# A hybrid decoder layer on one core: recurrence gates issued further behind their pair and one by one, and the silu gate's bank copied out before the sigmoid reads it

## The chip, the cores and the metric

The kernel runs on 1 core of one Trainium2 chip. The metric is the device time of one execution in microseconds (us); the times of a kernel are the median of several runs. One more execution was recorded by the hardware profiler, and its trace is what the views below read. The engines are TensorE (PE, with its weight load PEld), VectorE (DVE), ScalarE (ACT), GpSimd (POOL) and SyncE (SP, which issues nearly all DMAs).

## What is computed

One decoder layer on x (2048 x 1024) and 256 memory tokens, in float32. The reference, cut to the recurrence, which the change touches:

```python
hn = rms_norm(x, g_pre)
proj = hn @ w_in
rg_x, rg_g, da_q, da_k, da_v, da_g, xa_q, xa_g = jnp.split(proj, cuts, axis=-1)

xc = causal_depthwise_conv(rg_x, conv_w, conv_b)
r = sigmoid(xh @ w_rg_a + b_rg_a)
i = sigmoid(xh @ w_rg_x + b_rg_x)
log_a = -LRU_C * r * softplus(-lru_lambda)
u = sqrt(maximum(1 - exp(2 * log_a), 0)) * (i * xc)
h = scan(a * h + u)
y_rg = h * silu(rg_g)
...
y = jnp.concatenate([y_rg, y_da, y_xa], axis=-1) @ w_out
x = x + rms_norm(y, g_post)
```

Here xh is xc by heads. The other two groups are a differential attention (y_da) and a cross-attention into the memory tokens (y_xa), each times a silu gate.

## The kernel before, in words

Every float32 product is made of three matmuls (`mm3`, L197 through `mm`): each operand is split into a high part that TensorE's format holds and the low rest, and high x high, low x high and high x low are added in one PSUM bank. The function `split_weight` (L237, L238) does this for weights: ACT casts, POOL or DVE subtracts.

The 2048 tokens are four chunks of 512. The input projection (`project`, matmuls into tiles named `ip`) goes through 16 pairs of column blocks in two passes: chunks 0 and 1 in the first, chunks 2 and 3 in the second. A pair has four steps of 24 matmuls: for each of the two chunks one half and then the other. The tile `ip` lies in a PSUM pool of two banks, so a step needs the bank of the step before the last to be read out. In a recurrence pair ("rg", one for each of four blocks of 128 columns) the first half is the recurrence's input and the second its silu gate. In the first pass the four recurrence pairs come last, one after the other; in the second pass they alternate with attention pairs at places 1, 3, 5 and 7. So there are 16 places, one for each block and chunk.

After a step `ev_rg` takes the bank. For the first half ACT copies it (`xr`, L545), DVE runs the convolution of width 4 (`xc`, L550 and three times L553) and casts its high part (`xchl`, L556), and POOL subtracts to get the low part (L557). For the second half, the gate, ACT makes a sigmoid of three passes (Exp, Ln, Exp; L259 to L261) into `rgg`, and DVE multiplies it with the bank (L563). Then the generator `rg_gates` is handed to a list of streams. It makes the two recurrence gates: for each, three matmuls into a tile `rgo` from `xchl` and the split gate weights, and a sigmoid into `ri`. Then follow the recurrence's elementwise steps on ACT, POOL and DVE with a scan (L590), the multiply with `rgg` (L593) and a store that is issued 11 us later.

TensorE's order is the order in which the program issues its matmuls. It is set by a counter: `now[0]` grows by 512/2400 us for each matmul of 512 columns, streams carry a due time on that counter, and `pump`, called after every three projection matmuls, lets the due ones issue. `spawn(gen, delay)` puts a generator on the list, and each value that a generator yields is its next delay. The constant `RGW` is the delay between the end of a gate step and the first recurrence gate. The attention's streams (`s`, `pt`, `pthl`, `o`) and the transposes of the next rows (`xt`, `hnT`) run on the same list. For the other engines the framework sets the order, from priorities (`tc.high_priority`) and its own estimate of times; each engine then works through its list strictly in order, and what an instruction needs from another engine is a wait.

The `f2` tiles, among them `xr`, `xc`, `rgg`, the new `rgz` and the attention's `q2`, share nine buffers.

Of the kernel before, what the change touches and what calls it, by code (L numbers as in the profile page):

```python
# [18 lines left out]
CH = 512  # L19
# [12 lines left out]
S_GAP, SS_WAIT = 1.2, 6.25  # L32
XT_GAP, X1W = 1, 3.17
SQ0, SQ1, SQ_GAP = 0.1, 1.12, 1.39
RGW, XAW, XAT = 1.94, 1.77, 6.23

PRIO, PRS, PRX, PRN, PRM, PRR = 1000, 500, 500, 60, 261, -200
N_E = 12
# [19 lines left out]
def hybrid_layer(  # L58
# [13 lines left out]
    nc = tc.nc  # L72
# [16 lines left out]
    def f4(name, shape=(128, 1024), dt=F32, pool=p4):  # L89
        return pool.tile(list(shape), dt, tag="f4", name=name)  # L90

    def f2(name, shape=(128, 516), dt=F32, pool=p2):
        return pool.tile(list(shape), dt, tag="f2", name=name)
# [7 lines left out]
    def ps_s(name, shape=(128, 512)):  # L101
        return psS.tile(list(shape), F32, tag="S", name=name)
# [7 lines left out]
    def asf(ap):  # L110
        return ap.bitcast(F32)
# [92 lines left out]
    def spawn(gen, delay=0.0):  # L204
        streams.append([now[0] + delay, gen])

    def store(fn, delay):

        def go():
            fn()  # L210
            return
            yield
        spawn(go(), delay)
# [14 lines left out]
    def drain(cond=None):  # L228

        pump()  # L230
        while streams and not (cond is not None and cond()):
            now[0] = max(now[0], min(st[0] for st in streams))
            pump()
# [6 lines left out]
    def mm3(o, wh, wl, xh, xl, first, last):  # L240
        mm(o, wh, xh, first, False)
        mm(o, wl, xh, False, False)
        mm(o, wh, xl, False, last)
# [13 lines left out]
    def sigmoid(o, z, nb=0.0):  # L257

        nc.scalar.activation(o, z, AF.Exp, scale=-1.0, bias=nb)  # L259
        nc.scalar.activation(o, o, AF.Ln, bias=1.0)  # L260
        nc.scalar.activation(o, o, AF.Exp, scale=-1.0)  # L261
# [199 lines left out]
    def store_y(g, k, c, y):  # L461
        nc.sync.dma_start(YD[g][c][:, :, k, :].rearrange("t p k -> p t k"),
                          y.rearrange("p (t k) -> p t k", k=128))
# [64 lines left out]
    def rg_weights():  # L528
        raw = f4("rgraw", (128, 1024))
        nc.sync.dma_start(raw, w_rg)  # L530
        state["rgh"] = f4("rgh", (128, 4, 2, 128), F32R)
        state["rgl"] = f4("rgl", (128, 4, 2, 128), F32R)
        split_weight(raw, state["rgh"].rearrange("p a b c -> p (a b c)"),
                     state["rgl"].rearrange("p a b c -> p (a b c)"))

    def ev_rg(b, c, which, o):
        if which == 0:
            if c % 2:
                drain(lambda: not state["xa_live"])
            xr = f2("xr")  # L540
            if c == 0:
                nc.gpsimd.memset(xr[:, 0:3], 0.0)
            else:
                nc.gpsimd.tensor_copy(xr[:, 0:3], halo[:, b, :])
            nc.scalar.copy(xr[:, 3:515], o)  # L545
            if c < NCH - 1:
                nc.gpsimd.tensor_copy(halo[:, b, :], xr[:, 512:515])
            xc = f2("xc")
            cw = 4 * b
            nc.vector.tensor_scalar(xc[:, 0:CH], xr[:, 0:CH], vec2[:, cw:cw + 1], vec2[:, V_CB + b:V_CB + b + 1],  # L550
                                    op0=ALU.mult, op1=ALU.add)
            for k in range(1, 4):
                nc.vector.scalar_tensor_tensor(xc[:, 0:CH], xr[:, k:k + CH], vec2[:, cw + k:cw + k + 1],  # L553
                                               xc[:, 0:CH], op0=ALU.mult, op1=ALU.add)
            xh = f4("xchl", (128, 2, CH), F32R)
            nc.vector.tensor_copy(xh[:, 0], xc[:, 0:CH])  # L556
            nc.gpsimd.tensor_sub(xh[:, 1], xc[:, 0:CH], asf(xh[:, 0]))  # L557
            state["xc"] = xc, xh
            return
        xc, xh = state.pop("xc")  # L560
        gs = f2("rgg", (128, CH))
        sigmoid(gs, o)
        nc.vector.tensor_mul(gs, o, gs)  # L563
        state["rg_live"] = state.get("rg_live", 0) + 1
        spawn(rg_gates(b, c, xc, xh, gs), RGW)

    def rg_gates(b, c, xc, xh, gs):
        while state["xa_live"]:
            yield 0.5
        if "rgh" not in state:  # L570
            rg_weights()
            yield 5.0
        ri = f4("ri", (128, 2, CH))
        for g in range(2):
            o = ps_s("rgo")
            mm3(o, state["rgh"][:, b, g, :], state["rgl"][:, b, g, :], xh[:, 0], xh[:, 1], True, True)
            with tc.high_priority(offset=PRX):
                sigmoid(ri[:, g, :], o, nbias[:, 4 * g + b:4 * g + b + 1])
        with tc.high_priority(offset=PRR):
            r, i = ri[:, 0, :], ri[:, 1, :]  # L580
            a = f2("rga", (128, CH))
            nc.scalar.activation(a, r, AF.Exp, scale=nsp8[:, b:b + 1])
            nc.scalar.activation(r, r, AF.Exp, scale=nsp16[:, b:b + 1])
            nc.gpsimd.tensor_mul(i, i, xc[:, 0:CH])

            nc.vector.tensor_scalar(r, r, 1.0, 1.0, op0=ALU.min, op1=ALU.subtract)
            nc.scalar.activation(r, r, AF.Ln, scale=-1.0, bias=tinyb)
            nc.scalar.activation(r, r, AF.Exp, scale=0.5)
            nc.gpsimd.tensor_mul(i, i, r)
            nc.vector.tensor_tensor_scan(r, a, i, 0.0 if c == 0 else carry[:, b:b + 1], op0=ALU.mult, op1=ALU.add)  # L590
            if c < NCH - 1:
                nc.gpsimd.tensor_copy(carry[:, b:b + 1], r[:, CH - 1:CH])
            nc.vector.tensor_mul(r, r, gs)  # L593
        state["rg_live"] -= 1
        store(lambda: store_y(0, b, c, r), 11.0)
# [353 lines left out]
    def get_y(tt, grp):  # L949
        if (tt, grp) not in grans:  # L950
            drain(lambda: y_ready(tt, grp))
            grans[tt, grp] = y_granule(tt, grp)
        return grans[tt, grp]

    for tt in range(NT):
# [6 lines left out]
        for half, grp in order:  # L962
            cs = slice(half * 512, half * 512 + 512)
            g, wt = get_y(tt, grp), wout[grp]
            if os[half] is None:
                os[half] = ps_m("po")
            o = os[half]
# [82 lines left out]
```

## Time and profile before

| what | value |
|---|---|
| median of 3 runs | 1487.51 us (1486.01 to 1487.62) |
| the profiled execution | 1490.95 us |
| its span, first to last instruction | 1489.1 us |
| mean granted TensorE clock | 0.986 of 2.4 GHz |
| busy: PE / PEld | 1422.1 / 1208.6 us |
| busy: DVE / ACT / POOL | 918.4 / 811.5 / 563.8 us |
| DMA | 184.05 MB, 124 GB/s on average |

Busy time is the sum of an engine's instructions; on an engine that waits in line it says nothing of when. A list of waits shows for each line what ended the idle time before it. Matmuls overlap, so a row of the timeline with many of them gives their common duration. The granted clock is a share of 2.4 GHz, averaged over a stretch; the two levels are 1.2 and 2.4 GHz.

### The profile page before, as it was taken

The page shows a single profiled execution, that of the slowest core. Times are in us where ns is not written, and L with a number is a line of the kernel's source. Part 1 is how long each engine was busy: PE and PEld are TensorE (multiplying, and loading weights), DVE is VectorE, ACT ScalarE, POOL GpSimd, SP SyncE. Part 2 cuts the span into 40 slices and gives each one's busy share as a digit, 9 for nine tenths or more (in the row PEclk, how much of TensorE's full clock was granted, in tenths as well). Part 3 has the DMA queues.
Part 4 walks back from the last instruction along what each step waited for, and adds up shares of the span by engine and source line. Part 5 has one row for each costly group of instructions (what it writes and reads, how often), then busy time and mean ns, then how long its engine had stood idle before and what let it go on. Part 6 is the DMA issues. An engine that isn't in the chain of part 4 may idle for free.

```text
span 1489.1 us, 21951 instructions
## 1 busy us (share of the span) xinstructions
PE 1422.1 (95%) x7568; PEld 1208.6 (81%) x7568; DVE 918.4 (62%) x1862; ACT 811.5 (54%) x1972; POOL 563.8 (38%) x634
## 2 busy tenths in 40 slices
PE   5999999999998899899998999999999999999997
PEld 4789889888886678787786898888877888888886
DVE  6332565677545776757648576767778777777222
ACT  6343545666458674755556555666566545554221
POOL 2231433443446543535425343423346433334221
PEclk9999999999999899999999999999999999999999
DMA  6666666342322146244222543221375234322231
GB/s 218 162 214 219 177 172 206 99 132 82 106 68 64 50 128 187 72 151 123 84 68 71 163 141 128 68 85 40 116 237 174 86 133 151 103 96 76 99 123 70
DMA packets 138655, 184.05 MB, mean 124 GB/s; under 512 B 11440, under 2 KB 81200, under 8 KB 138544
## 3 DMA queue, kind: packets, MB, share of 16 engines
q1 hardware_dynamic: 138400, 182.64, 39.6%
q8 instruction: 59, 0.97, 0.3%
q14 instruction: 52, 0.43, 0.1%
q10 hardware_dynamic: 144, 0.01, 0.0%
HBM read 125.99 MB, written 56.62 MB: 123 GB/s over the span
## 4 chain that ended last, share of the span: by engine, by line
PE 74%; DVE 8%; ACT 6%; POOL 5%; issue 4%; DMA 2%; SPq 0%; DVEq 0%; POOLq 0%; ACTq 0%
PE ip L197 35%; PE po L197 17%; PE s L197 7%; PE o L197 6%; PE pt L201 4%; DVE e L719 2%; PE xas L197 2%; PE kv L197 1%; POOL e L718 1%; PE xao L197 1%; POOL wp L238 1%; DMA wraw<-in_w_in_dram 1%; PE rgo L197 1%; DVE xc L553 1%; ACT e L695 1%
## 5 line engine op out<-in xcount | busy, mean ns | idle before, releaser
L197 PE MATMUL ip<-hnT,wp 128*128 128x512 f32 x2688 | 676.8, 397 | 4.9 <-DVE rgg L563 4.9
L197 PEld LDWEIGHTS ip<-hnT,wp 128*128 128x128 f32 x2688 | 499.0, 190 | 105.8 <-DVE rgg L563 6.1
L695 ACT ACTIVATE e<-s,nm 128x512 f32<-128x512 f32 (+3 forms) x320 | 200.0, 625 | 233.4 <-DVE nm L693 216.3
L238 POOL TENSOR_TENSOR wp<-wraw,wp 128x512 fp32r<-128x512 f32 x133 | 182.2, 1380 | 201.8 <-ACT wp L237 192.8
L693 DVE TENSOR_REDUCE nm<-s 128x1 f32<-128x512 f32 (+3 forms) x320 | 193.2, 605 | 32.4 <-PE s L197 27.7
L197 PE MATMUL po<-wout,yg 128*128 128x512 f32 x768 | 193.5, 393 | 4.2 <-POOL wout L238 1.9
L718 POOL TENSOR_SCALAR e<-e,f 128x512 f32<-128x512 f32 (+3 forms) x160 | 120.3, 767 | 171.1 <-DVE f L714 93.5
L197 PE MATMUL s<-kv,q 128*128 128x512 f32 (+3 forms) x640 | 182.8, 367 | 1.0 <-ACT e L695 0.9
L197 PEld LDWEIGHTS po<-wout,yg 128*128 128x128 f32 x768 | 141.3, 188 | 34.3 <-POOL wout L238 3.3
L719 DVE SCALAR_TENSOR_TENSOR e<-e,f 128x512 f32<-128x512 f32 (+3 forms) x160 | 142.7, 919 | 28.5 <-POOL e L718 28.3
L197 PE MATMUL o<-pthl,kv 128*128 128x256 f32 (+1 forms) x864 | 136.3, 293 | 2.0 <-DVE pthl L760 2.0
L760 DVE TENSOR_TENSOR pthl<-pt,pthl 128x512 fp32r<-128x512 f32 (+1 forms) x144 | 94.6, 657 | 70.4 <-ACT pthl L759 70.0
L197 PEld LDWEIGHTS s<-kv,q 128*128 128x128 f32 x640 | 114.6, 189 | 21.8 <-ACT e L695 1.3
L197 PEld LDWEIGHTS o<-pthl,kv 128*128 128x128 f32 x864 | 116.1, 192 | 5.6 <-DVE pthl L760 2.8
L238 POOL TENSOR_TENSOR yg<-yraw,yg 128x512 fp32r<-128x512 f32 x48 | 64.2, 1341 | 133.1 <-ACT yg L237 122.0
L237 ACT CAST wp<-wraw 128x512 fp32r<-128x512 f32 x144 | 88.2, 618 | 43.9 <-PE ip L197 22.1
L759 ACT CAST pthl<-pt 128x512 fp32r<-128x512 f32 (+1 forms) x144 | 80.8, 561 | 53.3 <-PE pt L201 52.7
L197 PE MATMUL ip<-wp,hnT 128*128 128x256 f32 x768 | 99.4, 284 | 0.0
L197 PE MATMUL po<-wo,yg 128*128 128x512 f32 x384 | 97.3, 392 | 0.0
L197 PEld LDWEIGHTS ip<-wp,hnT 128*128 128x128 f32 x768 | 96.2, 192 | 1.2
L201 PE MATMUL pt<-ident,e 128*128 128x128 f32 x544 | 84.4, 276 | 5.6 <-DVE pthl L760 5.6
L201 PEld LDWEIGHTS pt<-ident,e 128*128 128x128 f32 x544 | 67.9, 142 | 20.8 <-DVE pthl L760 6.0
(183 smaller groups left out, 1731.2 us busy)
## 6 DMA issues: line engine op xcount, KB each, us to landing
wraw<-in_w_in_dram SPq DMA_DIRECT2D x128, 256.0 KB, 2.7
q<-QD SPq DMA_DIRECT2D x128, 128.0 KB, 3.3
kv<-KD SPq DMA_DIRECT2D x24, 512.0 KB, 5.7
kv<-VD SPq DMA_DIRECT2D x24, 512.0 KB, 5.0
yraw<-YD SPq DMA_DIRECT2D x48, 256.0 KB, 2.7
QD<-qkhl SPq DMA_DIRECT2D x32, 256.0 KB, 3.3
KD<-qkhl SPq DMA_DIRECT2D x32, 256.0 KB, 3.7
VD<-vhl SPq DMA_DIRECT2D x32, 256.0 KB, 2.8
```

The lines of the kernel that those rows point to most:

```text
L197: nc.tensor.matmul(o, w, xx, start=start, stop=stop)
L201: nc.tensor.transpose(o, i, ident)
L237: nc.scalar.copy(hi, raw)
L238: eng.tensor_sub(lo, raw, asf(hi))
L553: nc.vector.scalar_tensor_tensor(xc[:, 0:CH], xr[:, k:k + CH], vec2[:, cw + k:cw + k + 1], xc[:, 0:CH], op0=ALU.mult, op1=ALU.add)
L693: nc.vector.tensor_reduce(out=nm[:, c, kc:kc + 1], in_=s[:, 0:w], op=ALU.max, axis=AX.X, negate=True)
L695: nc.scalar.activation(e[kc, c][:, 0:w], s[:, 0:w], AF.Exp, bias=nm[:, c, kc:kc + 1], accum_out=l[:, c, kc:kc + 1])
L718: nc.gpsimd.tensor_scalar(e2, e2, f[:, 1, kc:kc + 1], 1.0, op0=ALU.mult, op1=ALU.mult)
L719: nc.vector.scalar_tensor_tensor(e1, e1, f[:, 0, kc:kc + 1], e2, op0=ALU.mult, op1=ALU.add)
L759: nc.scalar.copy(hi[:, 0:n], t[:, 0:n])
L760: nc.vector.tensor_sub(lo[:, 0:n], t[:, 0:n], asf(hi[:, 0:n]))
```

## The change

The first recurrence gate is issued after a delay of 5.0 instead of 1.94 on the counter, the second one after a further 1.4 instead of directly behind the first. The gate's bank is copied by DVE into a new SBUF tile `rgz`, and the multiply of the silu reads that copy and runs on POOL instead of DVE. Nothing else is edited; lines behind L563 move down by 1 to 3.

```diff
-RGW, XAW, XAT = 1.94, 1.77, 6.23
+RGW, RGG, XAW, XAT = 5.0, 1.4, 1.77, 6.23
...
         xc, xh = state.pop("xc")
-        gs = f2("rgg", (128, CH))
+        gs, z = f2("rgg", (128, CH)), f2("rgz", (128, CH))
+        nc.vector.tensor_copy(z, o)
         sigmoid(gs, o)
-        nc.vector.tensor_mul(gs, o, gs)
+        nc.gpsimd.tensor_mul(gs, z, gs)
         state["rg_live"] = state.get("rg_live", 0) + 1
         spawn(rg_gates(b, c, xc, xh, gs), RGW)
...
         ri = f4("ri", (128, 2, CH))
         for g in range(2):
+            if g:
+                yield RGG
             o = ps_s("rgo")
```

The change moves instructions on all engines. First TensorE, at the second recurrence pair of the first pass, second chunk. Before, six matmuls of two gates stand together behind twelve matmuls of the next step (`ip` with the buffer number of that step):

```order
L197 MATMUL ip_5155<-hnT01_318,wp_5012 128x512
L197 MATMUL rgo_5171<-xchl_5086,rgh_4787 128x512
L197 MATMUL rgo_5171<-xchl_5086,rgl_4788 128x512
L197 MATMUL rgo_5171<-xchl_5086,rgh_4787 128x512
L197 MATMUL rgo_5178<-xchl_5086,rgh_4787 128x512
L197 MATMUL rgo_5178<-xchl_5086,rgl_4788 128x512
L197 MATMUL rgo_5178<-xchl_5086,rgh_4787 128x512
L197 MATMUL ip_5155<-hnT00_317,wp_5096 128x512 x2
```

Now the first gate's three stand behind all 24 matmuls of that step, and a new `ip` tile begins behind them:

```order
L197 MATMUL ip_5163<-hnT01_318,wp_5118 128x512
L197 MATMUL rgo_5195<-xchl_5073,rgh_4801 128x512
L197 MATMUL rgo_5195<-xchl_5073,rgl_4802 128x512
L197 MATMUL rgo_5195<-xchl_5073,rgh_4801 128x512
L197 MATMUL ip_5219<-hnT00_317,wp_4958 128x512 x2
L197 MATMUL ip_5219<-hnT01_318,wp_4958 128x512
```

The first gate moved by twelve matmuls; the second one follows nine `ip` matmuls further on.

Second, DVE at the same place (`xc` is the convolution, `xrow` the rows of the next chunk, scaled by their norm). Before:

```order
L550 TENSOR_SCALAR xc<-xr,vec_179 128x512
L553 SCALAR_TENSOR_TENSOR xc<-xr,vec_179,xc 128x512 x3
L556 CAST xchl<-xc 128x512
L282 TENSOR_SCALAR xrow<-xrow,rs 128x512 x8
L563 TENSOR_TENSOR rgg<-ip,rgg 128x512
L586 TENSOR_SCALAR ri<-ri 128x512
```

Now:

```order
L553 SCALAR_TENSOR_TENSOR xc<-xr,vec_179,xc 128x512
L593 SCALAR_TENSOR_TENSOR ri<-rga,carry,ri 128x512
L553 SCALAR_TENSOR_TENSOR xc<-xr,vec_179,xc 128x512
L596 TENSOR_TENSOR ri<-ri,rgg 128x512
L553 SCALAR_TENSOR_TENSOR xc<-xr,vec_179,xc 128x512
L282 TENSOR_SCALAR xrow<-xrow,rs 128x512 x8
L556 CAST xchl<-xc 128x512
L562 COPY rgz<-ip 128x512
```

The eight scalings moved ahead of the cast, and the bank's copy stands behind the cast; the scan and the final multiply of the chunk before stand between the steps of the convolution.

Third, ACT at that place, with the semaphores that an instruction waits for. Before, the first pass of the sigmoid waits for TensorE:

```order
L274 ACTIVATE junk,ss<-xrows 128x512
L259 ACTIVATE rgg<-ip 128x512 [waits PE_49]
L274 ACTIVATE junk,ss<-xrows 128x512
L260 ACTIVATE rgg<-rgg 128x512 [waits Activation_49]
L237 CAST wp<-wraw 128x512 [waits DMAHW2_49]
L261 ACTIVATE rgg<-rgg 128x512 [waits Activation_49]
```

Now:

```order
L237 CAST wp<-wraw 128x512 [waits DMAHW5_49,PE_49]
L259 ACTIVATE rgg<-ip 128x512 [waits DVE_49]
L274 ACTIVATE junk,ss<-xrows 128x512 [waits DMAHW4_49,Pool_49]
L260 ACTIVATE rgg<-rgg 128x512 [waits Activation_49]
L274 ACTIVATE junk,ss<-xrows 128x512
L261 ACTIVATE rgg<-rgg 128x512 [waits Activation_49]
```

The first pass waits for DVE, whose copy reads the same bank.

Last, DVE at the last recurrence pair of the second pass, last chunk (`pthl` is the attention's transposed probabilities, L590 and L593 before are L593 and L596 now). Before:

```order
L550 TENSOR_SCALAR xc<-xr,vec_179 128x512
L590 SCALAR_TENSOR_TENSOR ri<-rga,carry,ri 128x512
L693 TENSOR_REDUCE nm<-s 128x1
L553 SCALAR_TENSOR_TENSOR xc<-xr,vec_179,xc 128x512
L593 TENSOR_TENSOR ri<-ri,rgg 128x512
L760 TENSOR_TENSOR pthl<-pt,pthl 128x512
```

Now:

```order
L589 TENSOR_SCALAR ri<-ri 128x512
L696 TENSOR_REDUCE nm<-s 128x1
L550 TENSOR_SCALAR xc<-xr,vec_179 128x512
L553 SCALAR_TENSOR_TENSOR xc<-xr,vec_179,xc 128x512
L763 TENSOR_TENSOR pthl<-pt,pthl 128x512
```

The scan and the multiply of the chunk before no longer stand ahead of `pthl`.

## Rows read from the trace of the kernel before

**Rows 1.** The page, busy time of each engine over the span.

```profile
PE 1422.1 (95%) x7568; PEld 1208.6 (81%) x7568; DVE 918.4 (62%) x1862; ACT 811.5 (54%) x1972; POOL 563.8 (38%) x634
```

**Rows 2.** TensorE's waits: waiting line, releaser, us in total, times, longest.

```profile
PE rgo L197 <- POOL xchl L557: 8.5, 6, 2.3
PE xt L201 <- DVE hnT L298: 5.9, 7, 1.4
PE pt L201 <- DVE pthl L760: 5.6, 1, 5.6
PE ip L197 <- DVE rgg L563: 4.9, 3, 2.8
PE rgo L197 <- DVE xchl L556: 3.3, 4, 1.1
```

**Rows 3.** Stretches: length, busy PE, PEld, DVE, ACT, POOL, clock, DMA, GB/s.

```profile
486.00:492.00 6.00, 6.00 (x16) 4.60 (x16) 4.35 (x6) 3.17 (x9) 3.19 (x4) 0.52 0.00 0
510.00:516.00 6.00, 3.54 (x9) 2.53 (x10) 4.03 (x4) 2.51 (x5) 5.20 (x5) 0.69 0.43 119
516.00:522.00 6.00, 6.00 (x22) 4.77 (x21) 3.24 (x5) 4.41 (x8) 2.34 (x5) 0.74 0.24 77
612.00:618.00 6.00, 5.26 (x19) 4.88 (x20) 2.86 (x7) 4.16 (x10) 1.93 (x2) 0.50 0.48 153
732.00:738.00 6.00, 4.36 (x13) 3.41 (x13) 4.32 (x3) 5.19 (x10) 5.17 (x5) 0.72 0.12 44
792.00:798.00 6.00, 2.28 (x11) 2.29 (x12) 5.99 (x6) 3.78 (x9) 4.19 (x3) 0.51 0.58 150
```

**Rows 4.** Timeline of TensorE: start, us, instruction, [idle time before it, releaser].

```profile
476.64 0.50 PE L197 MATMUL rgo<-xchl,rgh 128*128 128x512 f32 x1 [0.33 <-DVE xchl L556]
...
478.78 0.73 PE L197 MATMUL rgo<-xchl,rgh 128*128 128x512 f32 x2 [1.40 <-POOL xchl L557]
...
485.56 11.36 PE L197 MATMUL ip<-hnT,wp 128*128 128x512 f32 x36 [2.85 <-DVE rgg L563]
...
498.12 11.04 PE L197 MATMUL ip<-hnT,wp 128*128 128x512 f32 x48
510.24 0.50 PE L197 MATMUL rgo<-xchl,rgh 128*128 128x512 f32 x1 [1.08 <-DVE xchl L556]
...
513.19 1.22 PE L197 MATMUL rgo<-xchl,rgh 128*128 128x512 f32 x2 [2.21 <-POOL xchl L557]
```

**Rows 5.** Timeline of DVE at the same place.

```profile
475.25 1.33 DVE L556 CAST xchl<-xc 128x512 fp32r<-128x512 f32 x1
477.53 7.38 DVE L282 TENSOR_SCALAR xrow<-xrow,rs 128x512 f32<-128x512 f32 x8 [0.94 <-POOL rs L255]
...
496.15 3.26 DVE L282 TENSOR_SCALAR xrows<-xrows,rs 128x512 f32<-128x512 f32 x8 [3.19 <-POOL rs L255]
```

**Rows 6.** Timeline of POOL: the low half, and the last pair's row head.

```profile
477.45 1.28 POOL L557 TENSOR_TENSOR xchl<-xc,xchl 128x512 fp32r<-128x512 f32 x1
...
787.97 0.18 POOL L544 COPY xr<-halo 128x3 f32<-128x3 f32 x1
```

**Rows 7.** The tile `rgg`: min/median/max ns, first and last start, forms.

```profile
L259 ACT ACTIVATE rgg<-ip x16: 575/594/602, 433.8 to 792.7; 128x512 f32<-128x512 f32 x16
...
L563 DVE TENSOR_TENSOR rgg<-ip,rgg x16: 674/686/692, 435.7 to 799.0; 128x512 f32<-128x512 f32 x16
```

**Rows 8.** The tile `xc` on DVE, in the same form.

```profile
L553 DVE SCALAR_TENSOR_TENSOR xc<-xr,vec,xc x48: 720/752/1853, 428.0 to 797.3; 128x512 f32<-128x512 f32 x48
L550 DVE TENSOR_SCALAR xc<-xr,vec x16: 545/548/1101, 427.4 to 788.2; 128x512 f32<-128x512 f32 x16
L556 DVE CAST xchl<-xc x16: 395/427/1334, 430.3 to 798.0; 128x512 fp32r<-128x512 f32 x16
```

**Rows 9.** Timeline of DVE beside the last recurrence pair.

```profile
789.06 2.31 DVE L590 TENSOR_TENSOR_SCAN ri<-rga,carry,ri 128x512 f32<-128x512 f32 x1
...
794.98 0.68 DVE L760 TENSOR_TENSOR pthl<-pt,pthl 128x512 fp32r<-128x512 f32 x1
```

## The prediction, made before the change was run

> **What bounds the kernel now.** I read the page's busy shares first. TensorE is busy 95% of the span [rows 1], so the time is its own work plus whatever it waits. The work stays: no matmul is added or removed. The second view is the list of TensorE's waits [rows 2]. Three of its five lines belong to the recurrence: the gate matmuls `rgo` wait for the two halves of the convolved input, 8.5 us for the low half from POOL and 3.3 us for the high half from DVE, and the projection `ip` waits 4.9 us for a PSUM bank that the silu gate's last multiply (L563) still reads. A fourth, 5.6 us, is one wait for `pthl` beside the last recurrence pair. The third view is the granted clock in six short stretches [rows 3]: 0.50 to 0.74, where TensorE at 2.4 GHz shows 1.00; part of each stretch ran at 1.2 GHz. The fourth, TensorE's timeline, puts each dip right behind such a wait [rows 4]: 36 matmuls take 11.36 us behind the 2.85 us wait, where 48 take 11.04 us at full clock (0.23 us each).
>
> So a wait costs twice, as idle time and as slow work behind it. The slow part is the busy time of a stretch times what is missing of the clock [rows 3]: 0.48 x 6.00 + 0.31 x 3.54 + 0.26 x 6.00 + 0.50 x 5.26 + 0.28 x 4.36 + 0.49 x 2.28 = 2.9 + 1.1 + 1.6 + 2.6 + 1.2 + 1.1 = 10.5 us. What is at stake is 8.5 + 3.3 + 4.9 + 5.6 + 10.5 = 32.8 us.
>
> **Gates further behind.** The delays are polled after every three matmuls, each charged 512/2400 = 0.213 us, so 0.64 us a poll. 1.94 is reached at the fourth poll (12 matmuls), 5.0 at the eighth (24), 1.4 at the third (9); the order shows the same counts. The first gate is asked for 12 x 0.23 = 2.76 us later, the second 9 matmuls later still. Each place waits at the first gate alone: 1.08 us for the high half and then 2.21 us for the low half at 510 us, 3.29 together [rows 4]. This is the worst kind in the first pass; 2.76 us later, 0.5 us of it is left. The second pass has one alike, so I keep 1.0 us. Nothing is queued behind a gate on TensorE that needs it at once: the rest of the chain ends in a store issued 11 us later.
>
> **The place where this does not help.** In the second chunk of the second recurrence pair (476 us) the new order of DVE puts the eight row scalings L282 ahead of the high-half cast, and the copy of the gate's bank behind both. The scalings begin at 477.53 and took 7.38 us there; eight like them took 3.26 us at 496 us [rows 5]. The cast (0.43 us as a median [rows 8]) then ends at 481.2 to 485.3, and POOL's subtraction (1.28 us [rows 6]) at 482.5 to 486.6. TensorE asks for the low half at 476.31 + 2.76 + 2 x 0.23 = 479.5. The wait is 3.0 to 7.1 us; before, this place cost 0.33 + 1.40 + 2.85 = 4.6 us [rows 4]. I take the middle, 5.0, call the place unchanged, clock included, and keep -2.5 to +1.6 us for the range.
>
> So the removable part is 32.8 - 4.6 - 2.9 (its clock dip) = 25.3 us.
>
> **The copied bank.** Before, a gate's bank is held by three ACT passes and the multiply, 3 x 0.59 + 0.69 = 2.46 us if each pass takes what the first takes, queueing left out [rows 7]. Now DVE copies it, POOL multiplies the copy. The multiply that DVE loses pays for the copy: no copy from PSUM of this shape is in the trace; the nearest row from below is the convolution's first step, 0.55 us from SBUF [rows 8], from above the removed multiply, 0.69 us, which read the same bank. I take 0.69 and a gain of nothing on DVE. The order shows that the first sigmoid pass waits for DVE in all sixteen gates: copy and pass follow one another. The bank is then held 0.69 + 0.59 = 1.28 us, half of before, and I count the 2.05 us of bank waits outside the 476 us place (4.9 - 2.85) as gone. The rule that speaks against the edit stands in the Trainium skill, PSUM — Partial Sum Buffer, section "PSUM bank collisions raise a hardware error": two engines may not read one bank at once, and reads against reads count. By it the copy could not run "while" the sigmoid does, and the hold would be 1.28, not 0.69 us; the order agrees, no row here shows both reading.
>
> **The multiply on POOL.** Sixteen multiplies of two SBUF tensors, at 1.28 us (the subtraction of the same shape [rows 6]) 20.5 us more on an engine that is busy 38% [rows 1]. What they cost is DVE's time: its two-input step of the convolution takes 0.75 us as a median and up to 1.85 us [rows 8]. Bounds: 0 if no multiply meets such a step, 16 x (1.85 - 0.75) = 17.6 us of DVE time if each does. DVE is idle 38% of the span, and a step that is held up is on the path only near a gate. I take 2.0 us on the path. The Trainium skill, SBUF — State Buffer, section "Who interferes with whom", says why the maximum is so far above the median: a DVE instruction with two SBUF inputs and a POOL one that reads SBUF exclude each other. The trace agrees (0.75 against 1.85 us); the page alone would put the price at the upper bound whenever the two meet.
>
> **The wait beside the last pair.** DVE held `pthl` behind the scan of the previous chunk (789.06 us, 2.31 us), one step of the convolution and the final multiply, so that it started at 794.98 [rows 9]. In the new order the scan and the multiply stand behind it, and only the first step and one two-input step ahead. POOL delivers the row's head at 787.97 + 0.18 = 788.15 us [rows 6]; 0.55 + 0.75 (or 1.85) later [rows 8] `pthl` starts, at 789.5 to 790.6, 4.4 to 5.5 us sooner. Of 5.6 us that leaves 0.1 to 1.2; I take 1.2, since the attention's own steps share DVE there.
>
> **Also moved.** The transposes wait for `hnT` in 5.9 us in all [rows 2], partly where the first pass ends. DVE's list there is as long and TensorE comes sooner; I charge 1.5 us. The stores `YD<-ri` move with their chain on SP's queue and some weight loads pass them; the list of TensorE's waits has no line on a weight tile, so they have cover, and I charge nothing (if it is gone, a wait of the size seen here, 2 to 3 us a place [rows 4]). Of the clock I give back 1.3 us for the waits that stay.
>
> **Sum.** 25.3 - 1.0 - 2.0 - 1.2 - 1.5 - 1.3 = 18.3 us. The profiled execution took 1490.95 us (span 1489.1 and 1.85 around it): 1472.65. The median of the runs is 3.4 us below that execution, so I forecast 1469.2, rounded to **1469 us**.
>
> **Rivals.**
> - *Contention takes most of it.* Each POOL multiply holds up a two-input step, 17.6 us on DVE, half of it on the path: 8.8 instead of 2.0. The 476 us place is at its upper end, 2.1 us more. Gain 18.3 - 6.8 - 2.1 = 9.4, median 1478.1. For it: steps of 1.85 us are there already, and POOL's new multiply stands near the convolutions. Against: many multiplies fall where DVE reads PSUM.
> - *Slower, by ACT's queue.* The first pass now waits in ACT's queue for DVE, and behind it stand the copy of the next pair's input, the gates' own passes and the attention's exponentials. If two blocked steps (2 x 1.85 = 3.7 us [rows 8]) stand ahead of the copy, ACT stands 3.7 us, the next convolution starts so much later, and from 2.76 us on the new slack is used up: all waits come back, and the excess, 0.94 us, is added. At half the gates that is 7.5 us: median 1495. Against: DVE lists the copy mostly within two or three steps of the previous cast, and DVE no longer stands for ACT's third pass.
> - *The change moves the waits and does not shorten them.* If the scheduler puts the cast later at most places, as at 476 us, the high half is late by as much as the gates are: 1487.5. Against: at none of the other fifteen places does such a block stand between a convolution and its cast.
>
> **How the numbers follow.** My forecast, any gain from 12 to 27.8 us, has 0.62, with a range of its own of 1460 to 1475.5. Contention 0.16, ACT's queue 0.12, no change 0.10. A measurement of this kernel can tell about 0.2%, 3 us. Faster is 0.62 + 0.16 = 0.78; same 0.10; slower 0.12. The range runs from all of 25.3 and 2.5 us gone (1487.5 - 27.8 = 1459.7) up to the contention case with 6 us more, for a cover that is gone at two places, 1484; outside are slower and unchanged, 0.22.
>
> **What would show it.** TensorE's waits: `rgo` on `xchl` below 6 us in all, most of it at about 478 us; no `ip` wait on the copy elsewhere; `pthl` below 2 us. The clock at 1.00 in the stretches after 510, 612 and 732 us, still low near 485. L553's median should stay near 0.75 us; over 1.0 us would speak for contention. ACT idle before the gate's first pass, released by DVE, over 2.76 us at many gates would speak for the slower rival. The forecast is wrong if `rgo`'s waits stay near 11.8 us, or if a new line on `s`, `wp` or `hnT` takes their place.

## The result, and the profile after

The changed kernel takes 1498.99 us (median; 1496.1 to 1499.93), the kernel before 1487.57 us beside it. The ratio is 1.0075, 95% interval [1.0055, 1.0095]: slower by 11 us. The forecast was 1469 us; the range did not hold the time. The profiled executions are 7.6 us apart (1490.95 and 1498.58), since the one of the kernel before took 3.4 us more than its median; so the profiles below account for 7.7 us of span, and the runs for 11.4.

The changed kernel's page, busy time of each engine, answers to [rows 1]:

```profile
PE 1424.1 (95%) x7568; PEld 1208.2 (81%) x7568; DVE 919.8 (61%) x1862; ACT 811.4 (54%) x1972; POOL 579.7 (39%) x650
```

TensorE's busy time is up by 2.0 us, the span by 7.7. The other 5.7 us are idle time. Its waits, answering to [rows 2] (line, releaser, total, times, longest), cut to those that bear on the change; the largest other line, `xt` on `xrow`, is 13.6 us and was 14.1:

```profile
PE xt L201 <- DVE hnT L298: 14.6, 8, 7.2
PE rgo L197 <- DVE xchl L556: 4.4, 2, 4.0
PE s L197 <- ACT e L698: 4.1, 2, 2.8
PE o L197 <- DVE pthl L763: 4.1, 4, 2.4
PE s L197 <- DMA q<-QD: 2.0, 2, 1.8
PE rgo L197 <- POOL xchl L557: 1.5, 2, 0.7
PE ip L197 <- POOL wp L238: 1.3, 2, 1.0
PE ip L197 <- ACT rgg L259: 0.5, 1, 0.5
```

The three waits that the change aimed at did what the prediction said: `rgo` on `xchl` fell from 11.8 to 5.9 us, `ip` on the silu gate from 4.9 to 0.5, `pt` on `pthl` from 5.6 to nothing. In their place the transposes' wait for `hnT` rose by 8.7 us, two smaller lines grew (`s` on `e` from 0.9 to 4.1, `o` on `pthl` from 2.0 to 4.1) and two came (`q`, `wp`). That is one part of the account. The other is seen only when both kernels are cut at the same times. Stretches of the kernel before (length, busy PE, PEld, DVE, ACT and POOL, each but the first with its instructions, then clock, DMA share, GB/s):

```profile
420.00:560.00 140.00, 127.74 (x572) 102.67 (x572) 90.81 (x117) 98.85 (x197) 68.12 (x81) 0.95 0.27 80
560.00:825.00 265.00, 250.07 (x1270) 211.01 (x1269) 169.23 (x305) 154.20 (x343) 113.86 (x118) 0.97 0.37 109
825.00:1150.00 325.00, 316.67 (x1779) 270.87 (x1778) 231.72 (x461) 192.88 (x494) 132.57 (x149) 0.99 0.40 127
```

And of the changed kernel:

```profile
420.00:560.00 140.00, 121.64 (x536) 96.48 (x535) 86.25 (x108) 91.46 (x184) 76.49 (x86) 0.95 0.23 69
560.00:825.00 265.00, 254.31 (x1303) 215.03 (x1302) 174.08 (x314) 160.67 (x357) 124.80 (x129) 0.98 0.39 112
825.00:1150.00 325.00, 312.25 (x1745) 265.66 (x1744) 225.86 (x442) 189.07 (x485) 125.33 (x145) 0.99 0.39 125
```

Both programs have 7568 matmuls, so the count in a stretch is a ruler, a rough one, since the narrower matmuls take less time. The changed kernel does 36 fewer in the first pass's recurrence (420 to 560 us), wins 33 back in the second pass, and loses 34 between 825 and 1150 us, where no recurrence is left and no line of the change runs. The first two nearly cancel; at up to 0.23 us each, the 34 are about the 7.7 us by which it ends late.

**The place with the longest new wait.** TensorE of the changed kernel near 530 us, then the clock there:

```profile
522.78 1.64 PE L197 MATMUL ip<-hnT,wp 128*128 128x512 f32 x6
531.58 1.11 PE L201 MATMUL xt<-ident,xrow 128*128 128x128 f32 x4 [7.16 <-DVE hnT L298]
```

```profile
531.00:536.00 5.00, 4.42 (x15) 3.73 (x16) 3.24 (x4) 1.38 (x2) 1.97 (x3) 0.50 0.51 132
```

DVE, ACT and POOL of the changed kernel in that wait:

```profile
517.67 2.30 DVE L593 TENSOR_TENSOR_SCAN ri<-rga,ri 128x512 f32<-128x512 f32 x1 [5.62 <-POOL ri L592]
...
524.15 0.42 DVE L589 TENSOR_SCALAR ri<-ri 128x512 f32<-128x512 f32 x1
524.48 0.68 DVE L562 COPY rgz<-ip 128x512 f32<-128x512 f32 x1
529.60 1.28 DVE L593 TENSOR_TENSOR_SCAN ri<-rga,carry,ri 128x512 f32<-128x512 f32 x1 [4.44 <-POOL ri L592]
530.80 0.72 DVE L298 SCALAR_TENSOR_TENSOR hnT<-xt,vec,hnT 128x512 fp32r<-128x512 f32 x1
531.45 1.47 DVE L596 TENSOR_TENSOR ri<-ri,rgg 128x512 f32<-128x512 f32 x1
...
524.60 0.72 ACT L590 ACTIVATE ri<-ri,tinyb 128x512 f32<-128x512 f32 x1 [4.74 <-DVE ri L589]
525.23 0.61 ACT L260 ACTIVATE ri<-ri 128x512 f32<-128x512 f32 x1
...
526.27 0.61 ACT L261 ACTIVATE ri<-ri 128x512 f32<-128x512 f32 x1
...
526.96 1.26 POOL L587 TENSOR_TENSOR ri<-ri,xc 128x512 f32<-128x512 f32 x1 [1.26 <-ACT ri L261]
528.30 1.27 POOL L592 TENSOR_TENSOR ri<-ri 128x512 f32<-128x512 f32 x1
...
531.09 1.28 POOL L564 TENSOR_TENSOR rgg<-rgz,rgg 128x512 f32<-128x512 f32 x1
```

Read it backwards: `hnT` stands on DVE behind the scan; the scan waits for POOL's multiply L592, which stands behind L587; that waits for the second gate's sigmoid (L260 and L261), which stands in ACT's line behind L590 of the first gate; and L590 stood 4.74 us for DVE's L589, behind the next place's convolution. That convolution was late in its turn: DVE had stood 5.62 us, up to 517.67, for the scan of the place before. A kernel that is told of below (x1) has the first pass of the kernel before. There TensorE and DVE show the same group as:

```profile
527.32 0.60 PE L201 MATMUL xt<-ident,xrow 128*128 128x128 f32 x4
...
525.88 0.75 DVE L298 SCALAR_TENSOR_TENSOR hnT<-xt,vec,hnT 128x512 fp32r<-128x512 f32 x1
```

Against it TensorE of the changed kernel asks for this group 2.9 us sooner (at 524.42, which is 531.58 less the wait), and DVE starts `hnT` 4.9 us later.

### The profile page after: what moved, and what is told of

It reads as the page before. It is cut to its first block, busy times and chain, and to the rows that moved or that the text cites. A ratio compares the mean times of both kernels' runs of the same rounds, so it can differ in the third digit from the quotient of the medians.

```text
span 1496.8 us, 21973 instructions
## 1 busy us (share of the span) xinstructions
PE 1424.1 (95%) x7568; PEld 1208.2 (81%) x7568; DVE 919.8 (61%) x1862; ACT 811.4 (54%) x1972; POOL 579.7 (39%) x650
## 4 chain that ended last, share of the span: by engine, by line
PE 45%; DVE 9%; POOL 5%; ACT 5%; issue 5%; DMA 1%; SPq 0%; DVEq 0%; POOLq 0%; ACTq 0%
PE po L197 17%; PE ip L197 15%; PE s L197 5%; PE o L197 4%; PE pt L201 2%; DVE e L722 2%; POOL wp L238 1%; DVE xc L553 1%; DVE nm L696 1%; ACT e L698 1%; POOL ri L592 1%; POOL e L721 1%; DVE ri L593 1%; PE xas L197 1%; DVE pthl L763 1%
## 5 line engine op out<-in xcount | busy, mean ns | idle before, releaser
L722 DVE SCALAR_TENSOR_TENSOR e<-e,f 128x512 f32<-128x512 f32 (+3 forms) x160 | 145.8, 937 | 29.8 <-POOL e L721 29.3
L197 PEld LDWEIGHTS po<-wo,yg 128*128 128x128 f32 x384 | 71.0, 188 | 14.3
```

What stands on the lines that cost most here:

```text
L197: nc.tensor.matmul(o, w, xx, start=start, stop=stop)
L722: nc.vector.scalar_tensor_tensor(e1, e1, f[:, 0, kc:kc + 1], e2, op0=ALU.mult, op1=ALU.add)
```

## The experiments

Medians in us; "before" is the kernel before in runs on the same chip, 1486.8 to 1487.6 in all four groups.

### The change taken apart

The delays alone (`e1_delays_only`), the copy and the multiply on POOL alone (`e2_copy_only`), the first delay alone (`e3_first_delay_only`), and the change without the second delay (`e6_no_gap`):

```diff
# e1, against the changed kernel
-        gs, z = f2("rgg", (128, CH)), f2("rgz", (128, CH))
-        nc.vector.tensor_copy(z, o)
+        gs = f2("rgg", (128, CH))
         sigmoid(gs, o)
-        nc.gpsimd.tensor_mul(gs, z, gs)
+        nc.vector.tensor_mul(gs, o, gs)
# e6, against the changed kernel
-            if g:
-                yield RGG
# e3: both edits. e2: that of e6, and
-RGW, RGG, XAW, XAT = 5.0, 1.4, 1.77, 6.23
+RGW, RGG, XAW, XAT = 1.94, 1.4, 1.77, 6.23
```

> Only the two delays (5.0 and 1.4) are changed; the silu gate's bank is read by DVE's multiply as before. Theory 'late chain': the later gates push the recurrence's chain (ACT, DVE, POOL in turn) onto the in-order queues just where TensorE asks for the transposes' hnT, and the gates' gain is given back there; then this kernel loses nearly all that the change loses, 1495 to 1500 us, with an hnT wait of over 5 us near 525 us and hnT waits over 10 us in all. Rival 'bank copy': the copy and the multiply on POOL are what cost; then the delays alone are worth 5.9 us of rgo waits and the clock behind them, 1476 to 1482 us, and the hnT waits stay near 6 us in all. Rival 'reshuffle': the framework's order of the other engines falls out another way with every edit, and no part has the loss; then any time between, and the waits of the last third differ from both kernels.

> Only the bank's copy and the multiply on POOL; gates together and after 1.94 as before. Theory 'late chain': the gates stand where they stood, so no new hnT wait; the ip waits on L563 (4.9 us) go, the rgo waits stay near 11.8 us; 1483 to 1489 us. Rival 'bank copy': slower like the changed kernel or worse, 1495 to 1500 us, with the gate's chain behind ACT's wait for DVE's copy. Rival 'reshuffle': a time that neither explains, with waits after 825 us unlike both kernels.

> Only the first delay (5.0); the two gates stand together, the bank is read as before. Theory 'late chain' with the separation as its cause (the first gate's chain waits on ACT ahead of the second gate's passes): the 4.7 us wait of ACT's L587 for DVE in front of the second gate's passes near 520 us goes, hnT waits stay below 7 us in all, 1476 to 1483 us. Theory 'late chain' with the delay itself as its cause: hnT waits over 10 us and 1492 to 1500 us. Rival 'bank copy': 1476 to 1482 us, as for both delays.

> The changed kernel without the separation: first delay 5.0, gates together, bank copied and multiplied on POOL. If the separation is the cause: 1473 to 1482 us, the hnT wait of 7.2 us at 531 us gone. If the delay itself is: 1493 to 1500 us with that wait still over 4 us. If the copy is: 1493 to 1500 us, with hnT near 6 us in all and another wait in its place.

| kernel | median | ratio, 95% interval | rgo on xchl | ip on silu | hnT |
|---|---|---|---|---|---|
| delays alone | 1496.27 | 1.0062 [1.0046, 1.0079] | 0.2 | 10.0 | 12.9 |
| copy alone | 1507.29 | 1.0129 [1.0111, 1.0147] | 24.1 | 0 | 8.6 |
| first delay alone | 1506.77 | 1.0128 [1.0109, 1.0146] | 10.2 | 5.4 | 4.5 |
| change without second delay | 1516.06 | 1.0191 [1.0176, 1.0207] | 17.2 | 0 | 9.2 |

Every part alone is worse than before, and the parts don't add: the second delay takes 10.5 us off the first and 17 off the change. The first kernel came out as the late chain had it; for its time that was luck, since 6.5 of its 9.1 us are not there once the order of the other matmuls is kept (e8, in the next part). The other three left every range: the separation is no cause of the loss, without it the delay costs more, for a reason that no run shows; and the copy, which cost about 3 us on top of the delays, costs 20 by itself. TensorE and DVE of the kernel with the copy alone, at its longest wait:

```profile
487.21 0.80 PE L197 MATMUL rgo<-xchl,rgh 128*128 128x512 f32 x1 [6.01 <-DVE xchl L556]
...
478.52 0.69 DVE L562 COPY rgz<-ip 128x512 f32<-128x512 f32 x1 [0.43 <-PE ip L197]
480.56 6.26 DVE L282 TENSOR_SCALAR xrow<-xrow,rs 128x512 f32<-128x512 f32 x8 [1.35 <-POOL rs L255]
486.74 0.41 DVE L556 CAST xchl<-xc 128x512 fp32r<-128x512 f32 x1
```

At 487.21 TensorE had waited 6.01 us for that cast. The framework's list has the copy ahead of the cast at four of the sixteen places (the expectation for x6, further down, says five; it is four), and the cast then waits for the end of the gate's step. But that is not this wait: the copy was done at 479.21, and a cast of 0.41 us right behind it would have been ready before TensorE asked at 481.20. What made it late is the block of scalings, which the list now has ahead of the cast and which first stood 1.35 us for POOL. The next longest waits on the cast speak for the copy as little. At 622.15 us (4.16 us) the cast stands ahead of the copy, and at 464.22 us (3.73 us) a copy of 0.68 us stands between the steps of a convolution that was late itself, since DVE had stood 6.65 us for the scan of the place before. So the 20 us are shown; that the copy's own wait is their price is not, and these rows point to the new order of DVE's line instead.

### The counter

TensorE's order is made by a counter that each issued matmul advances. The gates' six matmuls advance it too, so moving them moves the due time of every stream behind. Without the `rgo` matmuls, the orders of TensorE in the two kernels are equal up to 532 us and then differ: about a third of the attention's matmuls stand 3 to 15 projection matmuls earlier or later, up to 1125 us and so well past the recurrence. Two edits keep one and move the other:

```diff
# e7, against the changed kernel; RGW is 1.94
+        now[0] += 6 * CH / 2400.0
+        yield RGF
         for g in range(2):
...
+            n0 = now[0]
             mm3(o, ...)
+            now[0] = n0
# e9, against the kernel before; its gates are not counted either
+        spawn(rg_count("rgh" not in state), RGC)
...
+    def rg_count(first):
+        while state["xa_live"]:
+            yield 0.5
+        if first:
+            yield 5.0
+        now[0] += 3 * CH / 2400.0
+        yield RGG
+        now[0] += 3 * CH / 2400.0
```

RGF is 2.2, RGG 1.4, RGC 5.0. `e8_counter_kept_no_copy` is e7 with the silu of e1, and `e10_gap_kept` is e8 without the line of RGF: only the second gate is late. In these three all 7472 matmuls but the gates' stand in the order of the kernel before; in `e9_counter_moved` they stand in that of the change.

> The changed kernel, but the counter that paces all streams advances where the gates stood before: the gates are issued as late and as far apart as in the change and are not counted there, so every other matmul of TensorE keeps the order of the kernel before. Theory 'counter': by 825 us, where the recurrence has ended, the changed kernel is 4.3 us ahead, and loses 12.0 us between there and 1146 us, since its attention's matmuls stand 3 to 18 places off against the projection's; then this kernel keeps about 4 us of lead to the end, loses less than 3 us after 825 us, and takes 1481 to 1488 us. Rival 'gates': the later gates and the bank's copy themselves cost, by DVE, ACT and POOL, whose order they change in the last third too; then 1495 to 1500 us, with the loss after 825 us still over 8 us.

> Both delays with the counter kept, the bank read as before (no copy, multiply on DVE). Theory 'counter': the delays alone were 0.5 us ahead at 825 us and lost 9 us after it; that loss goes, 1484 to 1490 us. Rival 'gates': 1493 to 1500 us.

> The kernel before with its gates where they stood and its bank read as before, but the counter advances where the change issues its gates: all other matmuls stand in the changed kernel's order, nothing else is changed. Theory 'counter': rgo waits stay near 11.8 us and the loss of 8 to 12 us after 825 us appears without any change of the gates, 1494 to 1501 us. Rival 'gates': 1486 to 1489 us, as before.

> The first gate where it stood, only the second one 9 matmuls later, counter kept, no copy. Where the first gate's wait for the high and then the low half is what costs, nothing is gained: 1485 to 1489 us. If the spread of the gates alone helps the chain behind (without it both the delay and the copy were 10 and 17 us worse), 1478 to 1485 us. If it hurts, since the second gate's sigmoid then stands behind ACT's wait for DVE, over 1490 us.

| kernel | median | ratio, 95% interval | matmuls, 825 to 1150 |
|---|---|---|---|
| before | 1486.83 | | 1779 |
| e7, gates late, copy, counter kept | 1492.46 | 1.0034 [1.0021, 1.0047] | 1782 |
| e8, the same, no copy | 1489.40 | 1.0019 [1.0008, 1.0030] | 1780 |
| e9, counter alone | 1491.90 | 1.0034 [1.0021, 1.0048] | 1748 |
| e10, second gate alone late | 1496.80 | 1.0068 [1.0054, 1.0081] | 1784 |

The stretch from 825 us of e9, where neither gates nor silu differ from the kernel before:

```profile
825.00:1150.00 325.00, 312.80 (x1748) 266.18 (x1747) 227.99 (x448) 188.71 (x484) 128.36 (x148) 0.99 0.40 125
```

and of e7, with the whole change except for the counter:

```profile
825.00:1150.00 325.00, 316.17 (x1782) 269.72 (x1781) 230.51 (x458) 192.53 (x495) 132.59 (x149) 1.00 0.41 128
```

The three kernels with the counter kept do as many matmuls there as before, e9 loses 31 and the change 34. The loss behind 825 us is the moved order and not the gates; the other engines' lists follow the order, and how much of the loss is theirs was not separated. e9's profile also does 24 matmuls more than before in the two stretches from 420 to 825 us, at a clock of 0.96 and 0.99 against 0.95 and 0.97, and so ends only 1.7 us late: what the order costs is told by the runs. By time e9 and e7 each missed their range by a few us, and e8 came within its own: the counter alone costs 5.1 us, and what is left without it costs 5.6. Taken off one after the other, the change's 11.4 us are 5.8 for the order (the change's excess over e7's), 3.1 for the copy (e7 against e8) and 2.6 for the late gates (e8, 1.2 to 4.5); taken off in another order the shares would differ, as the copy's 3 and 20 us show. Late gates do not pay even with the order kept. And e10 shows that a late second gate alone costs 10 us, as the third case of its expectation had it; its profile loses 33 matmuls between 560 and 825 us (1237 against 1270), where x1, in the next part, wins with both gates late. Why is not shown.

### Where late gates pay

Four kernels, all without the DVE copy: the bank copied by ACT with the gates as before (`x6_copy_on_act`), and with the counter kept late gates at all but the last three places of the first pass (`x2_not_at_pass_end`), in the second pass alone (`x1_second_pass`), and there with ACT's copy everywhere (`x1_second_pass_act`).

```diff
# x6, against e2
-        nc.vector.tensor_copy(z, o)
+        nc.scalar.copy(z, o)
# x1, against e8; in x2 late is c >= 2 or (b, c) < (2, 1)
+        late = c >= 2
-        yield RGF
-        for g in range(2):
-            if g:
-                yield RGG
+        if late:
+            yield RGF
+        for g in range(2):
+            if g and late:
+                yield RGG
```

> The gates stand as before (TensorE's order is that of the kernel before); the gate's bank is copied as in the change, but by ACT instead of DVE, and multiplied on POOL. With the copy on DVE this kernel took 1507.3 us, with rgo waits of 24.1 us. Theory 'cast behind copy': DVE's list has the copy ahead of the high-half cast at five of the sixteen places, and the copy can only run when TensorE has ended the gate's step, so the cast comes late; with the copy on ACT no cast stands behind one, the rgo waits fall back to 8 to 14 us, and the time to 1482 to 1491 us. Rival 'POOL multiply': sixteen multiplies of 1.3 us on POOL hold DVE's two-input steps and the low halves; they are still there, so the rgo waits stay over 18 us and the time over 1498 us.

> Both delays with the counter kept and no copy, but at the three places of the first pass that come last (second pair from the end, its second chunk, and the last pair) the gates stand as before. Theory 'pass end': the 8.2 us hnT wait near 535 us of the kernel with all places late comes from those places' chains in the queues of ACT, DVE and POOL; without them the hnT waits are near 6 us in all, the 7.1 us lag at 558 us falls to about 1, and the time from 1489.4 to 1482 to 1486 us. Rival 'earlier TensorE': TensorE asks for the transposes 2.5 us sooner since it no longer waits at the gates, and the wait only takes up what the gates gave; hnT waits over 9 us, 1487 to 1491 us.

> Both delays with the counter kept and no copy, in the second pass alone; the first pass is that of the kernel before. With all places late the lag fell by 7.3 us between 558 and 827 us, so if that stretch is worth the same from an undisturbed start: 1479 to 1484 us, rgo waits of the second pass under 1.5 us. If it only caught up what the first pass had made late: 1486 to 1490 us.

> The delays of the second pass alone with the counter kept, and the bank copied by ACT, multiplied on POOL, in both passes. If the copy on ACT is harmless and takes the ip waits on the multiply away: 1476 to 1483 us, no ip wait on L563's bank. If the multiply on POOL costs what the copy on DVE seemed to cost: over 1495 us.

| kernel | median | ratio, 95% interval | rgo on xchl | ip on silu | hnT |
|---|---|---|---|---|---|
| x6, ACT's copy, gates as before | 1493.28 | 1.0041 [1.0026, 1.0055] | 19.7 | 0 | 5.8 |
| x2, not at the pass's end | 1489.01 | 1.0012 [1.0000, 1.0023] | 6.6 | 11.3 | 5.3 |
| x1, second pass alone | 1481.54 | 0.9960 [0.9946, 0.9973] | 5.4 | 7.7 | 6.4 |
| x1 with ACT's copy | 1491.14 | 1.0024 [1.0013, 1.0034] | 11.8 | 0 | 6.8 |

The second pass alone is 5.6 us faster than before and beats both kernels; it came within its first range, and all its `rgo` waits on `xchl` are in the untouched first pass. x6 lies between its theories: 14 of the copy's 20 us go with the engine, but `rgo` stays at 19.7 us, as the rival said. At 476 us its cast is ahead of the scalings again and TensorE does not wait for it. Its longest wait on a cast, 5.05 us at 512.13, has steps of the convolution before it that took 5.00 us (2.33 at 486 us in the kernel before), beside subtractions of weights on POOL:

```profile
506.41 5.00 DVE L553 SCALAR_TENSOR_TENSOR xc<-xr,vec,xc 128x512 f32<-128x512 f32 x3
...
504.80 4.38 POOL L238 TENSOR_TENSOR wp<-wraw,wp 128x512 fp32r<-128x512 f32 x3
```

So neither "cast behind copy" nor "POOL multiply" is shown: the multiply on POOL was never run without a copy. With x1, ACT's copy and that multiply cost 10 us and miss both ranges. x2's time, 1489.0, is in the range of "earlier TensorE", but its `hnT` waits are not over 9 us: they went as the pass-end theory said, and a 7.83 us `ip` wait and 5.1 us of `rgo` waits stood in their place.

### Why not in the first pass

At 476 us stands the block of row scalings. Left out, with the gates as before (`z1_before_no_scaling`) and late (`z2_late_no_scaling`); the rows of chunks 2 and 3 then enter the second pass unscaled. `z3_first_pair_too` adds the first block's two places to x1. `z4_second_pass_counted` is x1 with the gates counted where they stand.

```diff
# z1, against the kernel before, and z2, against e8; scale is False for chunks 2 and 3
-            for i, row in enumerate(tiles):
+            for i, row in enumerate(tiles if scale else []):
# z3, against x1
-        late = c >= 2
+        late = c >= 2 or b == 0
# z4, against e1
-        spawn(rg_gates(b, c, xc, xh, gs), RGW)
+        spawn(rg_gates(b, c, xc, xh, gs), RGW if c >= 2 else 1.94)
...
-            if g:
+            if g and c >= 2:
```

> The kernel before without the sixteen scalings L282 of the rows of chunks 2 and 3 (they are left out, the rows go unscaled into the second pass). It is the base for the next run. At 476 us the cast and the multiply no longer stand by a block of 7.4 us: the 2.85 us ip wait goes, 1478 to 1486 us.

> All gates late, counter kept, no copy, and the sixteen scalings left out too. Theory 'scalings': their block is what the late chain runs into; without it the 7.8 us ip wait near 487 us and the 8.2 us hnT wait go or shrink below 4 us, and late gates gain in both passes: at least 5 us faster than the kernel before without scalings. Rival 'chains': the recurrence pairs follow one another without other work between them, and the late chain of one place meets the convolution of the next; then the hnT wait stays over 5 us, and the two kernels without scalings are within 3 us, as the two with them are (1489.4 and 1486.8).

> Second pass late and, in the first pass, the first pair's two places too, counter kept, no copy. Theory 'scalings': these two gates end before the block at 475 us, so nothing is lost and the 1.4 us ip wait at 455 us and the 0.4 us rgo wait may go: 1479 to 1483 us. Rival 'chains': the second place's chain now ends inside the next pair's convolution and the 7.8 us ip wait near 487 us comes back: 1485 to 1490 us.

> The second pass alone late, no copy, but counted where the gates now stand, as in the change. Theory 'counter': against 1481.5 us with the counter kept it loses the 5 us that the moved order cost by itself: 1484 to 1490 us, with the loss after 825 us. Rival: the moved order costs only together with the first pass's waits; 1479 to 1483 us.

| kernel | median | ratio, 95% interval |
|---|---|---|
| z1, no scalings, gates as before | 1485.46 | 0.9987 [0.9976, 0.9998] |
| z2, no scalings, gates late | 1485.95 | 0.9992 [0.9983, 1.0000] |
| z3, first pair late too | 1486.92 | 0.9994 [0.9985, 1.0003] |
| z4, second pass late, counted | 1484.77 | 0.9976 [0.9967, 0.9985] |

The scalings are not it alone: without them late gates gain nothing either (0.5 us between z1 and z2, as the rival "chains" had it), and z2 keeps `hnT` waits of 10.8 us. z1 came within its range. DVE's waits between 440 and 560 us, in z1:

```profile
DVE ri L590 <- POOL ri L589: 10.0, 6, 3.4
DVE rgg L563 <- ACT rgg L261: 4.4, 2, 3.6
```

and in z2, where the scan is L596:

```profile
DVE ri L596 <- POOL ri L595: 20.0, 6, 8.8
DVE rgg L563 <- ACT rgg L261: 18.8, 5, 8.3
```

With the scalings left in, the same two lines are 8.3 and 5.8 us in the kernel before and 9.5 and 9.8 in e8; there DVE stands for POOL's `rs` ahead of the scalings instead, 11.5 us (4.1 before).

In the first pass one recurrence pair follows the other with nothing between. A place's scan stands in DVE's line ahead of the next place's silu multiply or convolution; make its gates later, and DVE stands at the scan until they have come through ACT and POOL. Then the multiply is late, and with it TensorE's bank: what leaves `rgo` comes back as `ip` and `hnT`. z3 shows it at the smallest dose: two late places move 3.4 us out of `rgo` (5.4 to 2.0) and 3.9 into `ip` (7.7 to 11.6), and nearly all of x1's gain is gone. Its time is in the range of "chains", but the 7.8 us wait near 487 us did not come back (the longest is 3.9), and the idle time alone does not make the 5.4 us: from 420 to 560 us the profiles also show a clock of 0.95 in z3 and 0.99 in x1. z4 prices the counter a third time: about 3 us against x1, though the intervals of their two ratios overlap, with 1755 matmuls from 825 to 1150 us where x1 has 1794.

## Why the prediction was wrong, step by step

- **Gates further behind: right about its own wait, wrong about what is behind it.** `rgo` on `xchl` went below 6 us, as said. The step that failed is the sentence "Nothing is queued behind a gate on TensorE that needs it at once: the rest of the chain ends in a store". The rest of the chain is queued on ACT, DVE and POOL, ahead of the next place's convolution, silu multiply and `hnT`, and TensorE needs all three. At the longest new wait that chain held `hnT` and TensorE for 7.16 us. Most of the 18.3 us were to come from the late gates; with the order kept they cost 2.6 (e8), and in the second pass alone they gain 5.6 (x1).
- **A term was missing: the order of all other matmuls.** The change section showed the gates' rows alone, and the prediction gave the order of the other matmuls no term, though it set out how the counter grows with each matmul ("The work stays" is right of their number). The counter moved the order, for 5.1 us alone (e9), 5.8 in the change and about 3 on x1 (z4). No rival had it.
- **The 476 us place: right.** Counted as 5.0 us (3.0 to 7.1) with its clock dip: the cast's wait was 4.01 us at 481.87, and the clock 0.53 from 481 to 488 us. A wait of 1.02 us on `wp` at 476.44 comes on top.
- **The clock: right at its places, wrong in all.** The granted clock is 1.00 in the changed kernel from 510 to 522, 612 to 618 and 732 to 738 us, as said. But 10.5 - 2.9 - 1.3 = 6.3 us of clock were to come back, and the mean clock went from 0.986 to 0.987: new waits have slow stretches of their own behind them, 0.50 from 531 to 536 us and 0.72 from 690 to 697.
- **The copied bank: right in its durations, wrong in its place.** The copy took 0.680 us (0.69 was taken), and the `ip` waits on the silu went. But the step "a gain of nothing on DVE" priced the copy as busy time alone, where the edit also changed the order of DVE's line: on top of late gates the copy cost 3.1 us, with the gates as before 20. ACT's first pass stood for the copy at seven places, 10.9 us in all. The Trainium skill (PSUM — Partial Sum Buffer, "PSUM bank collisions raise a hardware error") says that two engines may not read one bank at once; the waits agree with it, and no run here shows two reading at once. A further trace of the copy, argued and not tried: in the changed kernel DVE's L550 stood 4.4 us at 467.57 for POOL's multiply L564, whose buffer the convolution takes over.
- **The multiply on POOL: sized right, its price is open.** 1.298 us as a median (1.28 was taken). The 48 two-input steps L553 took 47.2 us in all, before 49.6, at the same median of 0.752 us, so the sign that was named for contention did not come. Yet it moved elsewhere: the final multiply (L596, before L593) took 16.1 us, before 14.7, and in x6 18.9; at 531.45, beside L564, one took 1.47 us. The Trainium skill's rule (SBUF — State Buffer, "Who interferes with whom"), that a DVE instruction with two SBUF inputs contends with a POOL one that reads SBUF, agrees: in the kernel before each of the 16 steps L553 of over 1 us stands beside a POOL instruction of over 0.8 us, and of the 32 others three do; in the changed kernel it is 13 of 13, and one of 35. These are 1.4 us more of DVE's time; how much of the 2.0 us stands on the path is not shown, since no run has the multiply on POOL without a copy.
- **The wait beside the last pair: right for the wrong reason.** It went from 5.6 to nothing in the change, but the kernels with the counter kept still show 4.1 us; the gates gave 1.5 of the 4.4 us that were counted, the moved order the rest.
- **`hnT`: mis-sized.** 1.5 us were charged; it rose by 8.7, and 2.2 us of slow clock stand behind the longest wait (0.50 x 4.42).
- **Weights and stores: small, but not for the reason given.** Nothing was charged, 2 to 3 us a place if the cover is gone; TensorE's `ip` shows 1.3 us on `wp`, and `s` 2.0 on `q`. The sentence that the list of waits has no line on a weight tile is wrong: [rows 2] shows five lines of it, and further down it has 1.9 and 1.2 us on `wout` and 0.6 on `wp` (2.2, 1.6 and 0.5 in the changed kernel).
- **The rivals.** "Moves the waits and does not shorten them" (0.10) came nearest, for the first pass. The slower rival gave 1495 us, but by another mechanism: the 10.9 us that ACT stood for the copy are too few for it.

## What to carry to other kernels

Where a counter paces the program, an edit that moves a few instructions moves the due time of everything behind: compare the whole order without the moved rows, and try the edit with the counter kept before judging it. An operation that is asked for later takes its whole chain with it; look at what stands behind that chain's last wait on every in-order engine, above all where places follow one another without other work between. And an operation that is put on another engine can change the order of that engine's whole line: look at what stands ahead of the operation that the bottleneck waits for, not only at the new one's duration.

## What was not expected of the hardware

The clock behind a wait is not a fixed price. The kernel before and x1 have the same first pass and the same wait of 2.85 us in front of the same 36 matmuls, which took 11.36 us in the one [rows 4] and in x1:

```profile
486.08 8.45 PE L197 MATMUL ip<-hnT,wp 128*128 128x512 f32 x36 [2.85 <-DVE rgg L563]
```

In the six microseconds behind it the granted clock was 0.52 [rows 3] in the kernel before, 0.84 in e9 and 1.00 in x1:

```profile
486.00:492.00 6.00, 5.92 (x26) 4.92 (x27) 4.33 (x8) 3.61 (x11) 2.99 (x5) 1.00 0.00 0
```

So 2.9 of the 10.5 us that the prediction counted as the clock's need not be there in another execution. The runs of one kernel show it too: among the 33 of the kernel before beside z1 to z4, the fastest took 1483.37 us at a mean clock of 0.996 and the slowest 1491.35 us at 0.986. x1's gain is therefore told by its runs alone: its profile leads that of before by 9.3 us, its median by 5.6.
